# Two strip groups of the compression, and two levels of the gated recurrence, in one visit each of a hand-ordered matmul stream

## The chip, the cores and the metric

The kernel runs on one core of a Trainium2 chip, in one launch. The metric is the time of one execution on the device, in microseconds (us); less is better. Beside the times there is one profiled execution, whose records name every instruction by its engine, its line and its tiles.

## What is computed

A stack of two hybrid layers (three branches: sparse attention, gated linear attention, attention into a memory; then a gated merge and an MLP) and one further block, on 256 positions of width 1024, in float32. Two pieces of a hybrid layer matter here. The compression of the sparse attention's keys and values, cut to its core:

```python
raw = jnp.stack([split_heads(k_c, G), split_heads(v_c, G)])[:, :, :, cmp_idx]
raw = (raw + cmp_pe[:, None, None, None]).reshape(2, B, G, n_cmp, CMP_BLOCK * dh)
hid = jax.nn.gelu(jnp.einsum('kbgnf,kfe->kbgne', raw, cmp_w1))     # f is 2048, e is 256
comp = jnp.einsum('kbgne,ked->kbgnd', hid, cmp_w2)
```

and the attention matrix of the gated linear attention, in which each pair of positions i >= j is weighted by the decay between them:

```python
b = jnp.cumsum(ab, axis=2)
decay = jnp.exp(jnp.where(tril[:, :, None], b[:, :, :, None, :] - b[:, :, None, :, :], -jnp.inf))
attn = jnp.einsum('bhid,bhjd,bhijd->bhij', qb, kb, decay)
```

## The kernel before, in words

**The products.** A float32 product is made of three matmuls on a high and a low part of each operand (`mm3`, L194 and before it `mm`, L188, the one line that almost every matmul has in the trace). The weights stream from HBM in units of 512 KB: `unit` loads one into a raw buffer (tile `raw`, pool `wraw`, four buffers; the issue is on SP, L457), and `split` (L435 to L442) makes its high part `hi` on ACT (L441; every sixth unit on POOL, L439) and its low part `lo` on DVE (L442). The stationary operand of these products is the activation, the moving one a row block of weights 512 wide.

**The order on PE.** It is written by hand while the program is built. `tok_major` and `transposed` issue the big products; after each group of three matmuls they call `pump()`. All side work (recurrence, compression, scores, softmax products) is a set of generators, the chains. A chain issues a few instructions, then yields a number, the virtual time until it wants the next turn, a visit; `pump()` gives every chain whose time has come a visit, on a virtual clock that each matmul advances. So the numbers behind `yield` say where among the big products a visit falls. The order on ACT, DVE, POOL and SP is not written by hand: the framework's scheduler chooses it when the program is built. On every engine the instructions then run in their order, and a waiting instruction holds up all those behind it.

**The compression** (`nsa_cmp`, from L757). Tile `ph`, one bank of the pool `acc`, takes the product with `cmp_w1`. For each of two kinds (keys, values) there are four visits; each takes one raw buffer, fills it by two DMAs (L781) and issues four matmuls of 32 columns of stationary and 256 moving (L786), which occupy one strip of 32 columns each of the array. In a trace such a visit has eight records, since a float32 matmul goes in two passes. There are eight visits in each layer. These raw buffers come out of the same four as those of the big products, so a visit of the compression is what frees a buffer for a later weight unit.

**The gated recurrence** (`gla`, from L992). For each half of the positions (`tt`) ACT makes exponentials of prefix sums (PE products of `MLR` and `T` into a `psm` bank, L1021 on ACT into `E`, a `b8x` tile), DVE and POOL multiply keys and queries into them (L1025 to L1033 and `q_side`, L1048, which writes one of four tiles `QB`). Then come seven levels: each takes a bank of the pool `psm` (three banks, shared with every score, transpose and small product), issues two matmuls of 128 by 128 (four records) into its first half, and DVE copies the result under a mask into the matrix `A` (L1061); each level is a visit of its own. An eighth visit makes the diagonal (two matmuls of 2 columns, and the copy of L1073).

**What runs beside them.** In the stretch that matters most, the big products are first those of `gv` (columns 1816 to 2328 of `w_in`; their result is copied on ACT at L1286 into tile `g`), then those of `SR` (2328 to 2840, four weight units). Among them stand the first half of the recurrence, the compression, and the softmax of the sparse attention: scores on PE, a maximum on DVE (L899, L920), exponentials on ACT (L903, L924), normalisation on DVE (L905 to L929), transposes (L192 on PE).

Of the kernel before, what the change touches and what calls it, by code (L numbers as in the profile page):

```python
# [10 lines left out]
F32 = mybir.dt.float32  # L11
# [5 lines left out]
OP = mybir.AluOpType  # L17
AX = mybir.AxisListType.X

P = 128  # L20
# [18 lines left out]
CO_SEL = CO_TRIL  # L39
# [59 lines left out]
def block_kernel(ctx, tc, x_in, mem_in, positions, ln_mix, w_in, b_merge, nsa_q_norm, nsa_k_norm,  # L99
# [5 lines left out]
    nc = tc.nc  # L105
    act = nc.scalar.activation
    dve = nc.vector
    pool = nc.gpsimd

    consts = ctx.enter_context(tc.tile_pool(name="consts", bufs=1))  # L110
    wraw = ctx.enter_context(tc.tile_pool(name="wraw", bufs=NRAW))
# [10 lines left out]
    def nm(s):  # L122
        cnt[0] += 1
        return f"{s}_{cnt[0]}"

    LATF = 1.0
    clock = [0.0]
# [47 lines left out]
    def pe_time(ap, n):  # L175
        if ap.dtype == F32:
            return max(214.0, n * 1.69)
        return max(107.0, n * 0.425)

    def free(ap):  # L180
        n = 1
        for d in ap.shape[1:]:
            n *= d
        return n

    def mm(o, l, r, start, stop):
        clock[0] += pe_time(l, free(o))
        nc.tensor.matmul(o, l, r, start=start, stop=stop, skip_group_check=True)  # L188
# [35 lines left out]
    def A2(shape):  # L224
        return N2(shape, "a2")
# [10 lines left out]
    def PS():  # L236
        return psm.tile([P, 512], F32, tag="psm", name=nm("psm"))
# [7 lines left out]
    CF = consts.tile([P, CO_END], F32, name="CF")  # L245
# [17 lines left out]
    MASKS = consts.tile([P, MASK_W], U8, name="MASKS")  # L263
# [494 lines left out]
    def nsa_cmp(l, KD, GT, W2, T):  # L758
        R = [N2([P, 16, 2, 16]) for _ in range(2)]
# [13 lines left out]
        yield 3000.0  # L773
        ph = ACC()
        for k in range(2):
            for q in range(4):
                yield 3950.0
                raw = wraw.tile([P, 1024], F32, tag="raw", name=nm("raw"))
                rv = raw.rearrange("p (a n) -> p a n", a=4)
                for hl in range(2):  # L780
                    nc.sync.dma_start(rv[hl * 64:hl * 64 + 64],  # L781
                                      cmp_w1[l, k, hl * 1024 + q * 256:hl * 1024 + q * 256 + 256, :].rearrange(
                                          "(lp d) e -> d lp e", d=64))
                for j in range(4):
                    lp = 4 * q + j
                    nc.tensor.matmul(ph[32 * j:32 * j + 32, k * 256:k * 256 + 256],  # L786
                                     R[k][:, lp].rearrange("p a b -> p (a b)"), rv[:, j, :], start=q == 0,
                                     stop=q == 3, tile_position=(0, 32 * j), skip_group_check=True)
                clock[0] += 500.0
        cp = N2([P, 512])  # L790
        act(cp, ph, AF.Copy)
        yield 1500.0
# [1 line left out]
        for c in range(4):  # L794
# [4 lines left out]
                          op=OP.add, axis=AX)  # L799
# [186 lines left out]
    NQB = 4  # L986
    QB = [consts.tile([P, 2, 2, 64], F32, name=f"QB{i}") for i in range(NQB)]
# [3 lines left out]
    def gla(l, gq, gk, G, LOW, GLT, WG, o_gla, merged):  # L991
# [19 lines left out]
        for tt in range(2):  # L1011
            ts_ = slice(tt * P, tt * P + P)
            E = B8("b8x", shape=(2, 8, 128))
            for pr in range(2):
                for hf in range(2):
                    pd = PS()
                    rhs = MLR[:, 128 * tt + 512 * hf:128 * tt + 512 * hf + 512]
                    mm(pd, Th[:, tt, pr * P:pr * P + P], rhs, True, False)
                    mm(pd, Tl[:, tt, pr * P:pr * P + P], rhs, False, True)
                    yield 600.0  # L1020
                    act(E[:, pr, 4 * hf:4 * hf + 4, :].rearrange("p a b -> p (a b)"), pd, AF.Exp, scale=1.0 / 16)  # L1021
            for l2 in range(8):
                idx = l2 if tt == 0 else l2 + 1
                if idx == 0:
                    dve.tensor_tensor(KE, E[:, :, l2, :], gk[:, :, ts_], op=OP.mult)  # L1025
                elif idx == 8:
                    dve.tensor_tensor(E[:, :, l2, :], E[:, :, l2, :], gq[:, :, ts_], op=OP.mult)
                else:
                    s = 64 >> (idx - 1)
                    eng = dve if idx % 2 else pool  # L1030
                    e = E[:, :, l2, :].rearrange("p a (n u s) -> p a n u s", u=2, s=s)[:, :, :, 0, :]
                    q = gk[:, :, ts_].rearrange("p a (n u s) -> p a n u s", u=2, s=s)[:, :, :, 0, :]
                    eng.tensor_tensor(e, e, q, op=OP.mult)  # L1033
            yield 5350.0
            A = A2([P, 4, 128])
            AT.append(A)
            pool.memset(A, 0.0)

            def q_side(lev):
                sz = 64 >> (lev - 1)  # L1040
                qb = QB[(7 * tt + lev) % NQB]
                l2 = lev if tt == 0 else lev - 1
                eng = dve if lev % 2 else pool
                for j in range(2):
                    rr = slice(64 * j, 64 * j + 64)
                    e = E[rr, :, l2, :].rearrange("p a (n u s) -> p a n u s", u=2, s=sz)[:, :, :, 1, :]
                    q = gq[rr, :, ts_].rearrange("p a (n u s) -> p a n u s", u=2, s=sz)[:, :, :, 1, :]
                    eng.tensor_tensor(qb[rr, :, j, :].rearrange("p a (n s) -> p a n s", s=sz), e, q, op=OP.mult)  # L1048

            for lev in range(1, NQB + 1):  # L1050
                q_side(lev)
            for lev in range(1, 8):
                pa = PS()
                l2 = lev if tt == 0 else lev - 1
                qb = QB[(7 * tt + lev) % NQB]
                for pr in range(2):
                    mm(pa[:, pr * P:pr * P + P], E[:, pr, l2, :], qb[:, pr].rearrange("p j w -> p (j w)"),
                       True, True)
                sz = 64 >> (lev - 1)
                up_ = MASKS[:, None, 64 * (lev - 1):64 * lev].rearrange("p a (n s) -> p a n s", s=sz)  # L1060
                dve.copy_predicated(A.rearrange("p h (n u s) -> p h n u s", u=2, s=sz)[:, :, :, 1, :],  # L1061
                                    up_.to_broadcast([P, 4, 64 // sz, sz]),
                                    pa[:, 0:256].rearrange("p (h n s) -> p h n s", h=4, s=sz))
                if lev + NQB < 8:
                    q_side(lev + NQB)
                if lev == 1:
                    QK = E[:, :, l2, :]
                    pool.tensor_tensor(QK, gq[:, :, ts_], gk[:, :, ts_], op=OP.mult)
                yield 800.0
            pd = PS()  # L1070
            for pr in range(2):
                mm(pd[:, 2 * pr:2 * pr + 2], QK[:, pr, :], CF[:, CO_SEL:CO_SEL + 2], True, True)
            dve.copy_predicated(A, MASKS[:, None, 448:576].to_broadcast([P, 4, 128]),  # L1073
                                pd[:, 0:4, None].to_broadcast([P, 4, 128]))
            yield 1400.0
        Ac = A2([P, 4, 128])
        pas = [PS(), PS()]
# [32 lines left out]
        for hp in range(2):  # L1110
            pt = PS()
            for j in range(2):
                for tt in range(2):
                    h = 2 * hp + j
# [603 lines left out]
```

## Time and profile before

| | us |
|---|---|
| median of 3 runs | 1221.53 |
| the three runs | 1221.73, 1219.28, 1221.53 |
| the profiled execution, its own time | 1223.66 |
| span of its records | 1221.9 |
| PE busy (6553 matmul records) | 1201.4 |
| DVE busy | 871.5 |
| ACT busy | 605.1 |
| POOL busy | 199.5 |

A row of a timeline gives the start, the duration, the engine, the line, the operation with its tiles (numbers of buffers left out), the shapes, how many records stand together, and in brackets how long the engine had stood idle before it and what ended the wait. Matmuls overlap in the array: the pace of PE is read from one start to the next, not from the durations. Layer 1 shows the same pattern as layer 0, 472.0 us later.

### The profile page before, as it was taken

What the parts mean: (1) busy time and instruction counts of PE and PEld (TensorE: products, weight loads), DVE (VectorE), ACT (ScalarE), POOL (GpSimd) and SP (SyncE); (2) the same over time, 40 slices, a digit from 0 to 9 for tenths busy, and PEclk for the clock granted to TensorE, in tenths of its full rate; (3) what the DMA queues carried; (4) which work ended last, traced back from release to release, by engine and by line L of the source; (5) the groups of instructions that cost most, each with busy time, mean ns of one, the idle gap of its engine ahead of it and who ended that gap; (6) DMA issues with size and microseconds to landing.
All of it is one profiled execution on the core that took longest, in us unless ns stands there. A gap on an engine that the chain in (4) does not pass through costs nothing. (4 is left out here: it accounts for less than half of the span.)

```text
span 1221.9 us, 17759 instructions
## 1 busy us (share of the span) xinstructions
PE 1201.4 (98%) x6553; PEld 1004.8 (82%) x6553; DVE 871.5 (71%) x1457; ACT 605.1 (50%) x988; POOL 199.5 (16%) x235
## 2 busy tenths in 40 slices
PE   9999999999999999999999999999999999999997
PEld 6897777888788888888777888888888997998876
DVE  5977978677665656658868867665555799985677
ACT  7557544434645445466645444554554334443351
POOL 2310220120111112200312020121111111000201
PEclk9999999999999999999989999999999999999999
DMA  8567523676566666657613576656666555466662
GB/s 279 178 178 205 157 88 108 191 220 209 156 186 187 193 193 188 181 158 186 202 59 104 171 200 194 187 176 201 183 197 196 180 174 172 132 184 198 176 206 70
DMA packets 138699, 213.91 MB, mean 175 GB/s; under 512 B 12145, under 2 KB 76757, under 8 KB 138612
## 3 DMA queue, kind: packets, MB, share of 16 engines
q1 hardware_dynamic: 137284, 209.19, 57.8%
q0 software_dynamic: 1152, 3.31, 0.9%
q8 instruction: 51, 0.84, 0.3%
q14 instruction: 36, 0.29, 0.1%
q10 hardware_dynamic: 176, 0.27, 0.1%
HBM read 211.86 MB, written 1.05 MB: 174 GB/s over the span
## 5 line engine op out<-in xcount | busy, mean ns | idle before, releaser
L442 DVE TENSOR_TENSOR lo<-raw,hi 128x1024 fp32r<-128x1024 f32 (+1 forms) x369 | 458.6, 1246 | 219.9 <-ACT hi L441 169.4
L441 ACT ACTIVATE hi<-raw 128x1024 fp32r<-128x1024 f32 (+1 forms) x308 | 322.8, 1057 | 344.4 <-PE acc L188 284.5
L188 PE MATMUL acc<-hi,hx 128*128 128x512 f32 (+1 forms) x1024 | 338.3, 395 | 0.0
L188 PEld LDWEIGHTS acc<-hi,hx 128*128 128x128 f32 x1024 | 192.0, 189 | 40.2 <-issue 4.0
L188 PE MATMUL acc<-lo,hx 128*128 128x512 f32 (+1 forms) x512 | 197.3, 385 | 0.0
L439 POOL TENSOR_SCALAR hi<-raw 128x1024 fp32r<-128x1024 f32 x61 | 74.5, 1222 | 611.4 <-PE acc L188 438.5
L188 PE MATMUL acc<-hi,oh 128*128 128x512 f32 x400 | 157.9, 395 | 0.0
L188 PE MATMUL acc<-lo,oh 128*128 128x512 f32 x400 | 155.9, 390 | 0.0
L188 PE MATMUL acc<-hi,ol 128*128 128x512 f32 x400 | 155.8, 390 | 0.0
L188 PE MATMUL acc<-hx,hi 128*128 128x256 f32 (+1 forms) x704 | 137.7, 297 | 1.7 <-DVE hx L532 1.7
L188 PEld LDWEIGHTS acc<-hx,hi 128*128 128x128 f32 x704 | 110.9, 191 | 6.4 <-issue 2.3
L188 PE MATMUL psm<-hx,hi 128*128 128x512 f32 x448 | 111.8, 391 | 0.0
L188 PEld LDWEIGHTS acc<-lo,hx 128*128 128x128 f32 x512 | 96.9, 189 | 16.4
L188 PE MATMUL acc<-hi,b8x 128*128 128x512 f32 (+1 forms) x336 | 106.1, 388 | 1.4 <-ACT b8x L531 0.8
L188 PE MATMUL acc<-hx,lo 128*128 128x256 f32 x384 | 101.7, 284 | 0.3 <-DVE lo L442 0.3
L188 PEld LDWEIGHTS psm<-hx,hi 128*128 128x128 f32 x448 | 81.4, 189 | 15.1
L188 PEld LDWEIGHTS acc<-hi,ol 128*128 128x128 f32 x400 | 75.1, 188 | 15.9
L188 PEld LDWEIGHTS acc<-hi,oh 128*128 128x128 f32 x400 | 75.2, 188 | 14.7
L188 PEld LDWEIGHTS acc<-lo,oh 128*128 128x128 f32 x400 | 75.2, 188 | 14.6
L188 PEld LDWEIGHTS acc<-hi,b8x 128*128 128x128 f32 x336 | 62.3, 189 | 14.3 <-DVE b8x L532 1.5
L188 PEld LDWEIGHTS acc<-hx,lo 128*128 128x128 f32 x384 | 71.1, 191 | 1.5 <-DVE lo L442 0.5
L1351 POOL TENSOR_TENSOR tmp<-gtmp 128x512 f32<-128x512 f32 x32 | 39.1, 1223 | 165.7 <-ACT gtmp L1346 165.7
(359 smaller groups left out, 1464.4 us busy)
## 6 DMA issues: line engine op xcount, KB each, us to landing
raw<-in_w_in SPq DMA_DIRECT2D x160, 512.0 KB
raw<-in_w_up SPq DMA_DIRECT2D x64, 512.0 KB
raw<-in_w_down SPq DMA_DIRECT2D x64, 512.0 KB
raw<-in_w_branch SPq DMA_DIRECT2D x28, 512.0 KB
raw<-in_w_out SPq DMA_DIRECT2D x24, 512.0 KB
raw<-in_cmp_w SPq DMA_DIRECT2D x32, 256.0 KB
raw<-in_mem_w_kv SPq DMA_DIRECT2D x15, 512.0 KB
raw<-in_w_branch SPq DMA_DIRECT2D x16, 256.0 KB
```

The source lines that it names most:

```text
L188: nc.tensor.matmul(o, l, r, start=start, stop=stop, skip_group_check=True)
L439: pool.tensor_scalar(hi, raw, 1.0, 1.0, op0=OP.mult, op1=OP.mult)
L441: act(hi, raw, AF.Copy)
L442: dve.tensor_tensor(lo, raw, f32(hi), op=OP.subtract)
L1351: pool.tensor_tensor(u, r, r, op=OP.mult)
```

## The change

In the compression a visit now takes two raw buffers: it issues their four DMAs together, then the eight matmuls; a layer has four visits of eight matmuls in place of eight of four. The yield ahead of a visit becomes 8000 in place of 3950. In the recurrence the levels go in pairs (1, 2), (3, 4), (5, 6), and level 7 with the diagonal: a pair takes one `psm` bank, level 1 in its first half and level 2 in its second, then come the two masked copies one after the other; four visits in place of eight for each half, with yields of 1600, 1600, 1600 and 1400. The numbers of matmuls, copies and DMAs stay as they are.

```diff
--- before.py
+++ after.py
@@ -773,20 +773,24 @@
         yield 3000.0
         ph = ACC()
         for k in range(2):
-            for q in range(4):
-                yield 3950.0
-                raw = wraw.tile([P, 1024], F32, tag="raw", name=nm("raw"))
-                rv = raw.rearrange("p (a n) -> p a n", a=4)
-                for hl in range(2):
-                    nc.sync.dma_start(rv[hl * 64:hl * 64 + 64],
-                                      cmp_w1[l, k, hl * 1024 + q * 256:hl * 1024 + q * 256 + 256, :].rearrange(
-                                          "(lp d) e -> d lp e", d=64))
-                for j in range(4):
-                    lp = 4 * q + j
-                    nc.tensor.matmul(ph[32 * j:32 * j + 32, k * 256:k * 256 + 256],
-                                     R[k][:, lp].rearrange("p a b -> p (a b)"), rv[:, j, :], start=q == 0,
-                                     stop=q == 3, tile_position=(0, 32 * j), skip_group_check=True)
-                clock[0] += 500.0
+            for q2 in range(0, 4, 2):
+                yield 8000.0
+                rvs = []
+                for q in range(q2, q2 + 2):
+                    raw = wraw.tile([P, 1024], F32, tag="raw", name=nm("raw"))
+                    rv = raw.rearrange("p (a n) -> p a n", a=4)
+                    for hl in range(2):
+                        nc.sync.dma_start(rv[hl * 64:hl * 64 + 64],
+                                          cmp_w1[l, k, hl * 1024 + q * 256:hl * 1024 + q * 256 + 256, :].rearrange(
+                                              "(lp d) e -> d lp e", d=64))
+                    rvs.append(rv)
+                for q, rv in zip((q2, q2 + 1), rvs):
+                    for j in range(4):
+                        lp = 4 * q + j
+                        nc.tensor.matmul(ph[32 * j:32 * j + 32, k * 256:k * 256 + 256],
+                                         R[k][:, lp].rearrange("p a b -> p (a b)"), rv[:, j, :], start=q == 0,
+                                         stop=q == 3, tile_position=(0, 32 * j), skip_group_check=True)
+                clock[0] += 1000.0
         cp = N2([P, 512])
         act(cp, ph, AF.Copy)
         yield 1500.0
@@ -1049,29 +1053,33 @@
 
             for lev in range(1, NQB + 1):
                 q_side(lev)
-            for lev in range(1, 8):
+            for pair in ((1, 2), (3, 4), (5, 6), (7,)):
                 pa = PS()
-                l2 = lev if tt == 0 else lev - 1
-                qb = QB[(7 * tt + lev) % NQB]
-                for pr in range(2):
-                    mm(pa[:, pr * P:pr * P + P], E[:, pr, l2, :], qb[:, pr].rearrange("p j w -> p (j w)"),
-                       True, True)
-                sz = 64 >> (lev - 1)
-                up_ = MASKS[:, None, 64 * (lev - 1):64 * lev].rearrange("p a (n s) -> p a n s", s=sz)
-                dve.copy_predicated(A.rearrange("p h (n u s) -> p h n u s", u=2, s=sz)[:, :, :, 1, :],
-                                    up_.to_broadcast([P, 4, 64 // sz, sz]),
-                                    pa[:, 0:256].rearrange("p (h n s) -> p h n s", h=4, s=sz))
-                if lev + NQB < 8:
-                    q_side(lev + NQB)
-                if lev == 1:
-                    QK = E[:, :, l2, :]
-                    pool.tensor_tensor(QK, gq[:, :, ts_], gk[:, :, ts_], op=OP.mult)
-                yield 800.0
-            pd = PS()
-            for pr in range(2):
-                mm(pd[:, 2 * pr:2 * pr + 2], QK[:, pr, :], CF[:, CO_SEL:CO_SEL + 2], True, True)
-            dve.copy_predicated(A, MASKS[:, None, 448:576].to_broadcast([P, 4, 128]),
-                                pd[:, 0:4, None].to_broadcast([P, 4, 128]))
+                for i, lev in enumerate(pair):
+                    l2 = lev if tt == 0 else lev - 1
+                    qb = QB[(7 * tt + lev) % NQB]
+                    for pr in range(2):
+                        mm(pa[:, 256 * i + pr * P:256 * i + pr * P + P], E[:, pr, l2, :],
+                           qb[:, pr].rearrange("p j w -> p (j w)"), True, True)
+                if pair == (7,):
+                    for pr in range(2):
+                        mm(pa[:, 256 + 2 * pr:258 + 2 * pr], QK[:, pr, :], CF[:, CO_SEL:CO_SEL + 2], True, True)
+                for i, lev in enumerate(pair):
+                    sz = 64 >> (lev - 1)
+                    up_ = MASKS[:, None, 64 * (lev - 1):64 * lev].rearrange("p a (n s) -> p a n s", s=sz)
+                    dve.copy_predicated(A.rearrange("p h (n u s) -> p h n u s", u=2, s=sz)[:, :, :, 1, :],
+                                        up_.to_broadcast([P, 4, 64 // sz, sz]),
+                                        pa[:, 256 * i:256 * i + 256].rearrange("p (h n s) -> p h n s", h=4, s=sz))
+                    if lev + NQB < 8:
+                        q_side(lev + NQB)
+                    if lev == 1:
+                        QK = E[:, :, 1 if tt == 0 else 0, :]
+                        pool.tensor_tensor(QK, gq[:, :, ts_], gk[:, :, ts_], op=OP.mult)
+                if pair == (7,):
+                    dve.copy_predicated(A, MASKS[:, None, 448:576].to_broadcast([P, 4, 128]),
+                                        pa[:, 256:260, None].to_broadcast([P, 4, 128]))
+                else:
+                    yield 1600.0
             yield 1400.0
         Ac = A2([P, 4, 128])
         pas = [PS(), PS()]
```

How the built programs differ is seen on three engines at one place, in layer 0, where the products of `gv` end and those of `SR` begin. The lines of the changed kernel are shifted: L786 becomes L790, L1021 becomes L1025, L903 becomes L907, L924 becomes L928, L1286 becomes L1294.

On PE before, right behind the last products of `gv`: scores (`psm_1398`), a strip group of the compression (`acc_1066`), a product for the recurrence (`psm_1421`) and the first products of `SR` (`acc_1427`):

```order
L188 MATMUL psm_1398<-g_226_1219,b8x_1278 128x512
L188 MATMUL psm_1398<-g_227_1220,b8x_1278 128x512
L188 LDWEIGHTS CBT
L188 MATMUL psm_1398<-CBT 128x2x128
L786 MATMUL acc_1066<-raw_1413,n_192_1017 32x256 x4
L188 MATMUL psm_1421<-MLR,T_1270 128x512
L188 MATMUL psm_1421<-MLR,T_1271 128x512
L188 MATMUL acc_1427<-hi_1430,hx_135 128x512
L188 MATMUL acc_1427<-lo_1431,hx_135 128x512
```

and in the changed program:

```order
L188 MATMUL psm_1391<-g_226_1219,b8x_1271 128x512
L188 MATMUL psm_1391<-g_227_1220,b8x_1271 128x512
L188 LDWEIGHTS CBT
L188 MATMUL psm_1391<-CBT 128x2x128
L790 MATMUL acc_1066<-raw_1406,n_192_1017 32x256 x4
L790 MATMUL acc_1066<-raw_1409,n_192_1017 32x256 x4
L188 MATMUL psm_1421<-MLR,T_1263 128x512
L188 MATMUL psm_1421<-MLR,T_1264 128x512
L188 MATMUL acc_1427<-hi_1430,hx_135 128x512
L188 MATMUL acc_1427<-lo_1431,hx_135 128x512
```

Two strip groups stand together where one stood; the rest has its order. The fifth strip group of before, which stood 30 rows ahead of the one shown, is the first of the two here.

On ACT before, in the same stretch (`hi_1430` and `hi_1436` are the high parts of the first two units of `SR`, `pexp` the exponentials of the scores, `b8x` those of the recurrence, `g` the copies of `gv`):

```order
L751 ACTIVATE b8x_1278<-psm_1323,COL 128x4x128
L441 ACTIVATE hi_1430<-raw_1429 128x1024
L441 ACTIVATE hi_1436<-raw_1435 128x1024
L1021 ACT_TABLE_LOAD
L1021 ACTIVATE b8x_1369<-psm_1370 128x512
L903 ACTIVATE pexp_1355,s_248_1356<-psm_1346,n_246_1353 128x128 x4
L1021 ACTIVATE b8x_1369<-psm_1392 128x512
L924 ACTIVATE pexp_1382,s_256_1383<-psm_1376,n_254_1380 128x256 x2
L1286 ACTIVATE g_210_1182<-acc_1183,xrs_501 128x512
L1286 ACTIVATE g_210_1182<-acc_1184,xrs_501 128x512
L924 ACTIVATE pexp_1404,s_262_1405<-psm_1398,n_260_1402 128x256 x2
L441 ACTIVATE hi_1442<-raw_1441 128x1024
```

and in the changed program:

```order
L751 ACTIVATE b8x_1271<-psm_1323,COL 128x4x128
L1025 ACT_TABLE_LOAD
L1025 ACTIVATE b8x_1362<-psm_1363 128x512
L907 ACTIVATE pexp_1348,s_247_1349<-psm_1339,n_245_1346 128x128 x4
L1025 ACTIVATE b8x_1362<-psm_1385 128x512
L928 ACTIVATE pexp_1375,s_255_1376<-psm_1369,n_253_1373 128x256 x2
L1294 ACTIVATE g_210_1182<-acc_1183,xrs_501 128x512
L1294 ACTIVATE g_210_1182<-acc_1184,xrs_501 128x512
L928 ACTIVATE pexp_1397,s_261_1398<-psm_1391,n_259_1395 128x256 x2
L441 ACTIVATE hi_1430<-raw_1429 128x1024
L441 ACTIVATE hi_1436<-raw_1435 128x1024
L441 ACTIVATE hi_1442<-raw_1441 128x1024
```

The high parts of the first two units stood ahead of the table load and of all exponentials; they now stand behind them, with the third behind those two.

On DVE in the changed program, behind the normalisation of the scores (`pexp`; before, `lo_1431` stood ahead of the maximum of L899 and `lo_1437` ahead of the first of L920):

```order
L913 TENSOR_SCALAR pexp_1348<-pexp_1348,r_248_1354 128x128 x4
L924 TENSOR_REDUCE n_259_1395<-psm_1391 128x2
L930 RECIPROCAL r_256_1379<-s_255_1376 128x2
L931 TENSOR_TENSOR r_256_1379<-r_256_1379,GT_545 128x2
L933 TENSOR_SCALAR pexp_1375<-pexp_1375,r_256_1379 128x256 x2
L930 RECIPROCAL r_262_1401<-s_261_1398 128x2
L931 TENSOR_TENSOR r_262_1401<-r_262_1401,GT_545 128x2
L933 TENSOR_SCALAR pexp_1397<-pexp_1397,r_262_1401 128x256 x2
L442 TENSOR_TENSOR lo_1431<-raw_1429,hi_1430 128x1024
L442 TENSOR_TENSOR lo_1437<-raw_1435,hi_1436 128x1024
L442 TENSOR_TENSOR lo_1443<-raw_1441,hi_1442 128x1024
L442 TENSOR_TENSOR lo_1449<-raw_1447,hi_1448 128x1024
```

The low parts of the four units of `SR` now follow one another, behind the last normalisation. In layer 1 ACT has the same exchange, but for the first unit of `SR`, whose high part POOL makes before and now; its low part stands on DVE behind the first maximum and ahead of the normalisation.

## Rows read from the trace of the kernel before

**Rows 1.** The page, part 1: busy time, share of the span, instructions of each engine.

```profile
PE 1201.4 (98%) x6553; PEld 1004.8 (82%) x6553; DVE 871.5 (71%) x1457; ACT 605.1 (50%) x988; POOL 199.5 (16%) x235
```

**Rows 2.** The waits on PE: us in total, times, longest us.

```profile
PE psm L188 <- DVE a L1061: 2.1, 4, 1.3
...
PE psm L188 <- DVE tmp L798: 1.5, 2, 0.9
...
PE psm L192 <- DVE a L1061: 0.9, 1, 0.9
PE psm L192 <- DVE ck L834: 0.8, 1, 0.8
```

**Rows 3.** Timeline of PE, 114.4 to 116: start us, us, instruction, count of records.

```profile
114.40 0.40 PE L188 MATMUL acc<-hi,hx 128*128 128x512 f32 x1
114.73 0.64 PE L786 MATMUL acc<-raw,n 128*32 128x256 f32 x8
115.30 0.50 PE L188 MATMUL acc<-hi,hx 128*128 128x512 f32 x1
115.64 0.40 PE L188 MATMUL acc<-lo,hx 128*128 128x512 f32 x1
115.88 0.40 PE L188 MATMUL acc<-hi,hx 128*128 128x512 f32 x1
```

**Rows 4.** Timeline of PE: a level of the recurrence, and eight passes together.

```profile
137.34 0.61 PE L188 MATMUL psm<-QB,b8x 128*128 128x128 f32 x4
137.71 0.47 PE L188 MATMUL acc<-hi,hx 128*128 128x512 f32 x1
...
192.23 1.05 PE L188 MATMUL psm<-g,a 128*128 128x128 f32 x8
193.04 0.47 PE L188 MATMUL acc<-hi,hx 128*128 128x512 f32 x1
```

**Rows 5.** Timeline of PE, 119.5 to 121.9, where the products of SR begin.

```profile
119.54 0.39 PE L188 MATMUL acc<-hi,hx 128*128 128x512 f32 x1
...
120.22 0.28 PE L188 MATMUL psm<-CBT 128*128 128x256 bf16 x1
...
121.00 0.73 PE L188 MATMUL psm<-MLR,T 128*128 128x512 f32 x2
121.57 0.40 PE L188 MATMUL acc<-hi,hx 128*128 128x512 f32 x1
```

**Rows 6.** Timeline of ACT, 114 to 124.

```profile
114.03 2.00 ACT L441 ACTIVATE hi<-raw 128x1024 fp32r<-128x1024 f32 x2
...
118.00 0.36 ACT L903 ACTIVATE pexp<-psm,n 128x128 f32<-128x128 f32 x1
...
119.37 0.62 ACT L1021 ACTIVATE b8x<-psm 128x512 f32<-128x512 f32 x1
119.85 0.50 ACT L924 ACTIVATE pexp<-psm,n 128x256 f32<-128x256 f32 x1
...
120.75 1.31 ACT L1286 ACTIVATE g<-acc,xrs 128x512 f32<-128x512 f32 x2
121.89 0.53 ACT L924 ACTIVATE pexp<-psm,n 128x256 f32<-128x256 f32 x1
...
122.78 2.08 ACT L441 ACTIVATE hi<-raw 128x1024 fp32r<-128x1024 f32 x2
```

**Rows 7.** Timeline of DVE, 117 to 119.

```profile
117.64 1.22 DVE L442 TENSOR_TENSOR lo<-raw,hi 128x1024 fp32r<-128x1024 f32 x1
```

**Rows 8.** Line 1061 by itself: ns min/median/max, first and last start.

```profile
L1061 DVE COPY_PREDICATED a<-MASKS,psm x28: 416/432/741, 130.7 to 661.0; 128x256 f32<-128x256 uint8 x28
```

**Rows 9.** Timeline of PE, layer 1, the longest wait at a level.

```profile
652.33 0.68 PE L188 MATMUL psm<-QB,b8x 128*128 128x128 f32 x4 [1.25 <-DVE a L1061]
```

**Rows 10.** Stretches: us, busy time of PE, PEld, DVE, ACT, POOL; PEclk, DMA, GB/s.

```profile
631.00:638.00 7.00, 7.00 (x24) 4.93 (x24) 3.40 (x14) 1.50 (x3) 0.49 (x1) 0.52 0.01 2
638.00:675.00 37.00, 35.75 (x210) 28.68 (x210) 31.82 (x80) 19.99 (x46) 10.01 (x12) 1.00 0.31 92
```

## The prediction, made before the changed kernel ran

> **What bounds the kernel now.** I read the page first: PE is busy 98% of the span [rows 1], so the time is the length of PE's stream, and it changes only where PE issues something cheaper or dearer, or waits more or less. The page's chain of work that ended last covers only the last part of the span, so it says nothing on this change. Next the waits on PE: those that end at the recurrence and its neighbours are few, 2.1 us and 0.9 us for copies of levels (L1061), 1.5 us and 0.8 us for two vector operations of the compression (L798, L834) [rows 2]; 5.3 us in all for both layers. Then the timeline of PE at a visit of each kind, for its cost [rows 3, 4], and last the timelines of ACT and DVE where the new order differs most [rows 5 to 7]. Durations come from an execution whose own time was 1223.66 us (span 1221.9), 2.1 us above the median of 1221.53; I make a sum of differences and add it to the median. 0.2% is 2.4 us, about what a measurement of this kernel can tell from no change: 1219.1 and 1224.0 are the bounds.
>
> **Compression visits: -1.9 us.** Among plain products one start follows another after 0.24 us (115.64 to 115.88 [rows 3]). The visit at 114.73 comes 0.33 us after the start ahead of it, takes 0.57 us to the next start, and that product then needs 0.34 us [rows 3]: 0.09 + 0.57 + 0.10 = 0.76 us. Two visits cost 1.52 us. Merged, entry and exit are paid once: 0.19 saved. If an end of the last sweep, which is in the 0.57, is also paid once, and is of the size of the entry, 0.28 is saved. I take 0.24 for each of eight mergers in the two layers, -1.9 us, with ends -1.5 and -2.3. The DMAs stay the same in number and in SP's order; what changes is when a buffer comes free (below).
>
> **Recurrence visits: 0.** A level costs 0.37 us for four records to the next start, and that product runs some 0.08 long; eight records in a row cost 0.81 us [rows 4]. So two visits are 2 x 0.45 = 0.90, and a merged one 0.81 + 0.08 = 0.89. Sixteen banks saved save no PE time by themselves. Ends: 1 us either way, for neighbours that now meet. The vector copies are the same 28, of 0.43 us [rows 8], and 4 for the diagonal.
>
> **The wait that the change brings: +2.7 us in layer 0.** The raw buffers of the first units of SR come free when the compression has used them. Now two strip groups go together, so the first unit's buffer, which the third group frees before, is freed with the fourth, and the third unit's with the sixth instead of the fifth. The build answers by another order: the first two high parts, which ran on ACT at 114.03, in a gap ahead of the exponentials [rows 6], stand behind the exponentials, the two copies of gv and the last exponentials. ACT does its work in order, so SR waits for all of these. Step by step: three visits before this place (two mergers, and the group at 114.73, which is gone to the next visit) move the stream forward by 2 x 0.24 + 0.76 = 1.24 us. The exponentials hang on PE's scores, so they start at 118.00 - 1.24 = 116.8. From there to the last exponential ACT needs 122.78 - 118.00 = 4.78 us without a gap [rows 6], each of its sources being 1.24 us earlier too (the last products of gv, 119.54, and the last score, 120.22 [rows 5]). That is 121.5 or 121.6. The high part takes half of 2.08 us [rows 6]: 122.6. The low part on DVE takes 1.22 us [rows 7]: 123.8. PE wants the high part where SR starts, at 121.57 [rows 5] - 1.24 + 0.52 (the merged visit is 0.76 - 0.24 longer than one group) = 120.85, and the low part one product later. So it waits 1.75 us for the high part and, one product further, about 1.0 more for the low one: 2.7 us. The later units follow at 1.0 on ACT and 1.22 on DVE each, faster than PE uses one (twelve products of 0.24, 2.9 us), so they wait no more. Ends: 4.0 if ACT's block isn't pulled forward by the 1.24 us, and 0 if its exponentials run two to three microseconds ahead of my reckoning. I stay at 2.7, as PE's scores fix the start of the block.
>
> **The same place in layer 1: +0.2 us.** There POOL makes the first high part, and its low part is ahead of the normalisation. The second unit comes by the same reckoning at 122.6 for its high and 123.8 for its low part, on layer 0's scale (there the two copies of gv stand ahead of both score exponentials, which changes the order and not the sum). PE wants them 2.9 us and one more product for the recurrence (121.57 - 121.00 = 0.57 [rows 5]) after 120.85, at 124.3. Nothing or little is lost; ends 0 and 1.0.
>
> **The waits at the levels: 0.** The 5.3 us [rows 2] are banks and vector results that come late from DVE. Half as many banks are asked for, but each is held for two copies, with what DVE does between them. I see no reason for one to outweigh the other; ends -2.8 (half goes) and +4.3 (the rival below). PE being 2.7 us later in layer 0 gives DVE time there, yet DVE has four low parts in a row to make first.
>
> Sum: -1.9 + 0 + 2.7 + 0.2 + 0 = +1.0 us, **1222.5 us**.
>
> **The rivals.** *The waits shrink (faster).* If the exponentials run ahead so that SR waits only 1.0 us, and half of the waits at levels go with half of the banks, the sum is -1.9 + 1.0 + 0.2 - 2.8 = -3.5 us: 1218.0. For it: ACT is free of 2.00 us of high parts at 114.03 and DVE of a low part at 117.64 between its maxima [rows 6, 7]. Against it: the start of ACT's block is set by PE, not by ACT. Chance 0.22.
>
> *The shared bank is late (slower).* Waits for L1061 are five now, 3.0 us [rows 2]. A pair's bank comes free one masked copy later, and the build puts normalisations and a query product between the two copies. If each of the five waits grows by a copy and as much again, 2 x 0.43 [rows 8], that is +4.3, 1226.8. It decides from the point where PE asks for the third bank after a pair before DVE has done both copies; the longest wait, 1.25 us in layer 1 [rows 9], shows that DVE is that late at one place already. For it: DVE has four low parts in a row ahead of the first half's levels. Against it: only five waits stand behind 28 copies now [rows 2, 8], and half as many banks are asked for. Chance 0.20.
> The Trainium skill (Perfetto Trace Analysis, Optimizing Tensor Performance, Matmuls) says that independent groups of matmuls should rotate through different PSUM banks, so that the evacuation of one overlaps the matmuls of the next; two levels in one bank go against it. By that rule alone the time would be this rival's. The trace agrees in part: its waits for L1061 are waits for banks [rows 2], but most of the 28 copies [rows 8] held nobody up. So this rival has half the chance of the forecast.
>
> *The clock falls after the new gap (slower).* After the small matmuls of layer 1 the granted clock is 0.52, the level of 1.2 GHz, for 7.0 us, and 1.00 again after that [rows 10]: 3.4 us lost. If the gap of 2.7 us ahead of SR brings half to one such stretch, 1222.5 + 1.7 to + 3.4, 1224.2 to 1225.9. Against it: the clock is 1.00 over the stretch from 638 that holds the wait of 1.25 us [rows 9, 10]. Chance 0.10.
>
> *The merger doesn't merge (slower).* If the second strip group of a visit waits for its own DMA, or four strips on the next buffer begin anew, entry and exit are paid twice and the 1.9 us don't come: 1222.5 + 1.9 = 1224.4. Chance 0.08. The forecast keeps 0.40.
>
> **How the numbers follow.** The forecast lies within 0.2% of 1221.53: same, 0.40. The first rival is faster: 0.22. The others are slower: 0.20 + 0.10 + 0.08 = 0.38. The low end, 1217.8, stands just below the price of the faster rival, which leaves out its lower half, 0.11; the high end, 1227.0, just above the price of the late bank, which leaves out its upper half, 0.09.
>
> **What would show it right or wrong.** Right: the visit of the compression has 16 records within some 1.14 us and four visits in a layer; ACT's high part of SR's first unit follows the last exponentials of the scores; the first two products of SR in layer 0 stand with waits for ACT's L441 and DVE's L442, together 2 to 4 us, and layer 1 has no such pair; waits for the copies of levels (now L1070) stay near 3 us. Wrong: no wait at the first product of SR in layer 0; waits for L1070 above 6 or below 1 us; a row of PEclk near 0.5 right after the start of SR.

## The result, and the profile after

The changed kernel takes 1232.55 us (median of 4 runs, 1230.0 to 1234.11) against 1221.63 for the kernel before beside it: a ratio of 1.0075, 95% interval 1.0057 to 1.0094. It is slower by some 11 us, and the forecast was 1222.5, with a range up to 1227.0. Slower had the chance of 0.38, but the size was far off. The profiled execution has a span of 1230.8 us, 8.9 more than before; its account is made below.

The page of the changed kernel, part 1, answers to [rows 1]:

```profile
PE 1203.1 (98%) x6553; PEld 1007.5 (82%) x6553; DVE 871.1 (71%) x1457; ACT 604.8 (49%) x988; POOL 192.4 (16%) x235
```

PE has the same 6553 records and still 98% of the span. The waits on PE in the changed kernel (us in total, times, longest us), answering to [rows 2], leaving out waits outside the two hybrid layers' attention stages:

```profile
PE psm L192 <- ACT b8x L1025: 3.1, 1, 3.1
PE psm L192 <- DVE pexp L933: 2.5, 2, 1.2
PE acc L188 <- ACT hi L441: 1.8, 1, 1.8
...
PE psm L192 <- ACT pts L945: 1.7, 2, 0.9
PE psm L188 <- ACT n L813: 1.3, 2, 1.1
...
PE acc L188 <- DVE lo L442: 1.2, 3, 0.8
...
PE psm L188 <- DVE a L1070: 0.7, 3, 0.3
PE pso L188 <- ACT pts L674: 0.7, 1, 0.7
...
PE psm L192 <- DVE ck L838: 0.6, 1, 0.6
PE psm L188 <- ACT b8x L1025: 0.5, 2, 0.2
```

Waits for the masked copies of the levels were 3.0 us (L1061 [rows 2]) and are 0.7 now (L1070). What came instead are waits for ACT (L1025, L441, L945, L813) and for normalised exponentials from DVE (L933). The ten rows make 14.1 us; 0.4 of the row for L442 lies elsewhere, so 13.7 stand in the two stages, where before there were 5.6 ([rows 2], and one of 0.3 for L941).

The place in layer 0 that the prediction worked out, on PE and on ACT (timelines; [rows 5, 6] before):

```profile
120.06 0.28 PE L188 MATMUL psm<-CBT 128*128 128x256 bf16 x1
120.28 1.07 PE L790 MATMUL acc<-raw,n 128*32 128x256 f32 x16
121.28 0.74 PE L188 MATMUL psm<-MLR,T 128*128 128x512 f32 x2
123.81 0.50 PE L188 MATMUL acc<-hi,hx 128*128 128x512 f32 x1 [1.79 <-ACT hi L441]
125.06 0.50 PE L188 MATMUL acc<-lo,hx 128*128 128x512 f32 x1 [0.76 <-DVE lo L442]
```

```profile
117.84 0.36 ACT L907 ACTIVATE pexp<-psm,n 128x128 f32<-128x128 f32 x1
...
121.73 0.53 ACT L928 ACTIVATE pexp<-psm,n 128x256 f32<-128x256 f32 x1
...
122.62 2.07 ACT L441 ACTIVATE hi<-raw 128x1024 fp32r<-128x1024 f32 x2
```

The visit has 16 records in 1.00 us. PE comes here a microsecond later than reckoned, in part by a wait of 0.7 us for L674 in the stretch ahead, and with it the exponentials (117.84, forecast 116.8) and the high part (122.62, forecast 121.6); the first two products of SR wait 1.79 and 0.76 us. That is the 2.7 of the forecast, at 2.55.

In layer 1 the start of SR has no such wait, but another follows some four microseconds behind it. ACT, PE and SP there:

```profile
598.60 2.08 ACT L441 ACTIVATE hi<-raw 128x1024 fp32r<-128x1024 f32 x2
603.66 1.06 ACT L441 ACTIVATE hi<-raw 128x1024 fp32r<-128x1024 f32 x1 [2.98 <-DMA raw<-in_w_in]
604.62 1.06 ACT L1025 ACTIVATE b8x<-psm 128x512 f32<-128x512 f32 x2
```

```profile
601.71 0.49 PE L192 MATMUL psm<-CF,pexp 128*128 128x128 f32 x3
605.25 0.90 PE L192 MATMUL psm<-CF,pexp 128*128 128x128 f32 x3 [3.05 <-ACT b8x L1025]
```

```profile
586.47 10.86 SPq L457 DMA_DIRECT2D raw<-in_w_in  x4
597.43 4.85 SPq L783 DMA_DIRECT2D raw<-in_cmp_w  x4
```

ACT makes the high parts of SR's second and third unit at 598.60 and is then to make the fourth. Its transfer is the last of the four that SP issues by 597.33 (586.47 + 10.86), right ahead of four transfers of the compression; it lands at 603.66, when ACT's wait for it ends. ACT waits 2.98 us for it. Behind it in ACT's order stand the two copies out of PSUM banks for the recurrence (L1025 at 604.62). The transposes on PE need one of the three banks, and wait 3.05 us for the copy to free it.

The transfer is late because its buffer is. Before, SP had issued the same four units by 588.48, 5.0 us ahead of SR's first product at 593.46:

```profile
575.94 12.54 SPq L457 DMA_DIRECT2D raw<-in_w_in  x4
```

Now the last goes out by 597.33, 0.5 us ahead of SR's first product at 597.83. SP issues the third unit at 594.84, after a wait for the first unit's own low part (L442), and the fourth at 596.96, after a wait of 1.7 us for the merged visit of 596.26 (L790). In layer 0 it waits 9.5 us for such a visit ahead of the third.

The third part is the granted clock (stretches, columns as in [rows 10]). Of the changed kernel:

```profile
122.00:126.00 4.00, 1.45 (x6) 0.99 (x6) 3.27 (x7) 3.84 (x8) 0.00 (x0) 1.00 0.79 261
126.00:131.00 5.00, 5.00 (x27) 4.17 (x26) 4.90 (x9) 2.33 (x4) 4.36 (x6) 1.00 0.93 206
160.00:168.00 8.00, 8.00 (x33) 5.97 (x33) 5.33 (x21) 2.30 (x10) 1.14 (x2) 0.57 0.20 66
596.00:602.00 6.00, 6.00 (x40) 4.39 (x39) 5.60 (x17) 4.68 (x12) 0.00 (x0) 1.00 0.96 250
604.00:612.00 8.00, 6.75 (x23) 4.83 (x23) 5.30 (x11) 2.06 (x4) 4.70 (x8) 0.57 0.56 158
642.00:646.00 4.00, 4.00 (x15) 2.38 (x15) 2.90 (x13) 2.30 (x10) 1.14 (x2) 0.58 0.32 117
```

and the first low stretch of the kernel before, whose second one is in [rows 10]:

```profile
159.90:163.40 3.50, 3.50 (x13) 2.23 (x13) 1.95 (x9) 1.40 (x3) 0.00 (x0) 0.52 0.00 0
```

Before, 3.5 and 7.0 us at 0.52 cost 10.5 x 0.48 = 5.0 us. Now it is 8 us at 0.57, 8 at 0.57 and 4 at 0.58: 8.6 us lost, 3.6 more. The one from 604 is new, and begins within PE's wait of 3.05 us.

So the profiled execution adds up: 13.7 - 5.6 = +8.1 of waits, +3.6 of clock, and the merged visits of the compression, 0.33 us for each of eight (1.00 instead of 2 x 0.57 inside, and the 0.19 of one entry and exit, an estimate taken over from before), -2.6. Sum +9.1, against 8.9. Two things stand outside this sum: the other waits of PE are 1.0 us less in all (one of 0.8 us for L531 is gone), and the first 1.25 us of the low stretch from 604 lie within PE's wait, so that some 0.5 us is counted twice. With both, 7.6 of the 8.9 us are accounted for.

### The profile page after: what moved, and what is told of

The parts are those of the page before. It is cut to its first block, busy times and chain, and to the rows that moved or that the text cites. A ratio compares the mean times of both kernels' runs of the same rounds, so it can differ in the third digit from the quotient of the medians.

```text
span 1230.8 us, 17763 instructions
## 1 busy us (share of the span) xinstructions
PE 1203.1 (98%) x6553; PEld 1007.5 (82%) x6553; DVE 871.1 (71%) x1457; ACT 604.8 (49%) x988; POOL 192.4 (16%) x235
## 5 line engine op out<-in xcount | busy, mean ns | idle before, releaser
L442 DVE TENSOR_TENSOR lo<-raw,hi 128x1024 fp32r<-128x1024 f32 (+1 forms) x369 | 458.3, 1245 | 230.2 <-ACT hi L441 177.2
L441 ACT ACTIVATE hi<-raw 128x1024 fp32r<-128x1024 f32 (+1 forms) x308 | 322.7, 1057 | 349.7 <-PE acc L188 287.9
L188 PEld LDWEIGHTS acc<-hi,b8x 128*128 128x128 f32 x336 | 62.4, 189 | 13.7 <-DVE b8x L532 1.5
```

The source lines that it names most:

```text
L441: act(hi, raw, AF.Copy)
L442: dve.tensor_tensor(lo, raw, f32(hi), op=OP.subtract)
```

## The experiments

Each execution's records give its span and its mean granted clock. To tell waits from clock I put beside each median the mean of span x granted clock over the runs of that kernel, an estimate of the time that it would take at the full clock. The kernel before ran again beside each group, and each ratio is to the kernel before of its own group.

| kernel | median us | ratio to before, interval | mean granted clock | span x clock, us |
|---|---|---|---|---|
| before (35 runs beside the third group) | 1222.49 | | 0.9959 | 1215.6 |
| changed, once more | 1230.50 | 1.0064 (1.0050 to 1.0079) | 0.9928 | 1219.7 |
| pairs of levels alone | 1224.29 | 1.0011 (1.0001 to 1.0021) | 0.9947 | 1216.0 |
| pairs of strip groups alone | 1228.25 | 1.0040 (1.0027 to 1.0053) | 0.9934 | 1218.6 |
| changed, pairs of groups early | 1225.93 | 1.0023 (1.0007 to 1.0039) | 0.9945 | 1217.8 |
| early pairs of groups alone | 1227.67 | 1.0036 (1.0024 to 1.0049) | 0.9948 | 1219.9 |
| changed, one high part of layer 1 on POOL | 1230.01 | 1.0069 (1.0052 to 1.0085) | 0.9923 | 1219.6 |
| changed, one of layer 0 on POOL | 1231.69 | 1.0070 (1.0054 to 1.0086) | 0.9903 | 1218.2 |
| changed, both on POOL | 1230.25 | 1.0061 (1.0042 to 1.0080) | 0.9937 | 1220.3 |
| outer pairs of groups alone | 1223.01 | 1.0009 (0.9994 to 1.0023) | 0.9958 | 1216.0 |
| outer pairs of groups, pairs of levels | 1221.62 | 0.9991 (0.9977 to 1.0005) | 0.9952 | 1213.9 |
| changed, five raw buffers | 1218.36 | 0.9977 (0.9966 to 0.9989) | 0.9958 | 1212.0 |
| before, five raw buffers | 1223.83 | 1.0020 (1.0009 to 1.0030) | 0.9939 | 1214.9 |
| pairs of groups alone, five raw buffers | 1220.95 | 0.9984 (0.9975 to 0.9993) | 0.9954 | 1213.6 |
| pairs of levels alone, five raw buffers | 1223.54 | 0.9998 (0.9989 to 1.0007) | 0.9964 | 1216.9 |

Theory A: the pairs of strip groups free the buffers of SR's weight units late, so splits and transfers come late, and engines that work in order hold other work up behind them. Theory B, the rival of the prediction: the shared bank of two levels makes the waits.

### The halves of the change

Each half alone: the loop of the other is that of the kernel before.

```diff
-            for pair in ((1, 2), (3, 4), (5, 6), (7,)):
+            for lev in range(1, 8):
...
```

> The pairs of levels alone; the compression as before. Theory A (the loss comes from the paired strip groups, which free the weight buffers later, so that splits move behind other work on ACT and DVE): no wait at the first product of SR, no 3 us wait for L1021 in layer 1, time within 2 us of before (1219.5 to 1223.5). Theory B (the shared bank of two levels, held for two copies, makes the waits): most of the loss is here, 1227 to 1232, with the waits at transposes and small products of the first half of the recurrence as in the changed kernel (together over 5 us a layer).

> The paired strip groups alone; the levels of the recurrence one by one as before. Theory A: all or most of the loss is here, 1228 to 1233, with waits of 1.8 and 0.8 us at the start of SR in layer 0 and some 3 us for L1025 in layer 1. Theory B: little of it, 1219 to 1224.

The pairs of levels cost 1.0 us (before was 1223.29 in this set), the pairs of groups 5.0. Waits on PE of the pairs of groups alone:

```profile
PE psm L188 <- DVE a L1065: 3.4, 4, 1.2
PE psm L188 <- ACT ck L831: 2.2, 2, 1.7
...
PE acc L188 <- ACT hi L441: 1.8, 1, 1.8
```

Theory A holds for the larger part: the wait of 1.8 us at the start of SR is there with the pairs of groups alone. The wait of 3 us for L1025 in layer 1 is not (0.5 us); there other small waits stand, for L1065 and L831. The halves don't add up either: 1.0011 and 1.0040 against 1.0064 to 1.0075. Theory B is refuted as the main cause.

### Earlier visits

```diff
-                yield 8000.0
+                yield 4000.0 if k == 0 and q2 == 0 else 8000.0
```

> The changed kernel, but with the first of the four paired strip visits of a layer 4000 instead of 8000 of virtual time after its predecessor, so that a pair stands about where the first of its two groups stood before and its two weight buffers come free earlier, not later. Theory A: the waits at the start of SR and for L1025 in layer 1 go, and with them 6 us or more: 1220 to 1226. Theory B: the levels are paired as in the changed kernel, so it stays at 1229 to 1234.

> The paired strip groups alone, at the early places; levels one by one. Theory A: the merger's saving of some 2 us without the waits, 1217 to 1221. Theory B: the same as before less 2 us, 1218 to 1221, and 8 us or more below the early pairs with paired levels.

With the levels in pairs the waits at the start of SR are gone and the time is 1225.93, at the upper end of what theory A said; with the levels one by one it is 1227.67, far above its 1217 to 1221. Theory B's 1218 to 1221 is missed there too. So theory A in this form is not enough. The early visits seem only to have turned the late buffer round, as the waits on PE of the second show:

```profile
PE acc L790 <- DMA raw<-in_cmp_w: 3.0, 2, 1.9
PE psm L192 <- DVE ck L838: 2.4, 2, 1.9
```

Now the visit itself is early for its own transfers (3.0 us in two waits), since its two buffers must be free at one time, and the chain behind the compression is late (2.2 us for L802 and 2.4 for L838, where the kernel before has 1.5 and 0.8 for the same lines, L798 and L834 [rows 2]).

### The changed kernel again, and single instructions moved

The first run repeats the changed kernel. The others move one high part each to POOL:

```diff
-        if u % 6 == 5:
+        if u % 6 == 5 or u == 176:
```

Unit 176 is SR's fourth in layer 1; u == 30 is SR's first in layer 0; both together are the fourth run.

> The changed kernel once more, for a second profile and beside the next three on one chip. If the 3 us wait for L1025 in layer 1 and the stretch of low granted clock that begins in it belong to the program, both are there again, and the time is 8 to 11 us above before. If the stretch of low clock was chance, the wait is there without it and the time is 5 to 8 us above before.

> The changed kernel with one instruction moved: the high part of SR's fourth unit in layer 1 is made on POOL instead of ACT, so that ACT no longer waits for that unit's transfer ahead of the copy out of the PSUM bank. Order of PE and DVE unchanged. If this convoy on ACT makes the 3 us wait: the wait for L1025 falls below 0.5 us, the time by 3 us, and by 3 more where the low clock came with the gap: 3 to 7 us below the changed kernel. If PE would wait there anyway (for the low part of the unit, or the bank through another holder): within 1 us of it.

> The changed kernel with the high part of SR's first unit in layer 0 on POOL, as layer 1 has it; the build then puts its low part ahead of the normalisation on DVE. If the place behind ACT's exponentials makes the wait at the start of SR: the waits of 1.8 and 0.8 us go and the time falls by 2 to 3 us. If the unit's transfer is what is late, the wait stays, on POOL's L439: within 1 us.

> Both moves. If the two waits are separate pieces of the loss: 5 to 9 us below the changed kernel, 1 to 5 above before. If the loss moves on to later waits (DVE and ACT behind): less than 3 us below the changed kernel.

The repeat is 7.8 us above before (1222.72 in this set), just under the 8 to 11 expected, and its wait for L1025 and its low clock in layer 1 are there again, both somewhat smaller:

```profile
PE psm L192 <- ACT b8x L1025: 2.3, 1, 2.3
```

```profile
604.00:608.50 4.50, 3.65 (x11) 3.04 (x12) 4.13 (x9) 1.66 (x4) 3.48 (x6) 0.62 0.99 266
```

None of the three moves gains anything clear of the noise. With the fourth unit of layer 1 on POOL, the wait of 3 us for L1025 is gone, and another takes its place. Waits on PE, then POOL and DVE:

```profile
PE pso L188 <- DVE pts L947: 2.4, 1, 2.4
```

```profile
604.48 1.04 POOL L439 TENSOR_SCALAR hi<-raw 128x1024 fp32r<-128x1024 f32 x1 [11.32 <-DMA raw<-in_w_in]
```

```profile
605.55 1.47 DVE L442 TENSOR_TENSOR lo<-raw,hi 128x1024 fp32r<-128x1024 f32 x1 [1.90 <-POOL hi L439]
```

POOL now waits for the transfer (until 604.48), DVE for POOL's high part (1.90 us, until 605.55), and a copy behind that on DVE's order (L947) is what PE waits for. So ACT was only the engine that happened to carry the late transfer; the transfer is the cause of this wait. With SR's first unit of layer 0 on POOL the waits of 1.8 and 0.8 us go, and waits for L1025 and L813 come in the same layer (over both layers, on PE):

```profile
PE psm L192 <- ACT b8x L1025: 4.2, 2, 2.9
PE psm L188 <- ACT n L813: 2.8, 2, 1.7
```

In this kernel ACT makes the fourth unit's high part ahead of the copy L1025 in layer 0 too. The loss moves on: theory A's first, narrow reading, that two instructions stand at the wrong place, falls. The reading left is that buffers come free late, and somebody waits wherever the splits are put.

### Which pairs, and more buffers

Only groups 1 and 2, and 7 and 8 in pairs; 3 to 6 single, as their visits free SR's buffers:

```diff
-            for q2 in range(0, 4, 2):
-                yield 8000.0
+            for qs in (((0, 1), (2,), (3,)), ((0,), (1,), (2, 3)))[k]:
+                yield 8000.0 if len(qs) == 2 else 3950.0
```

> Levels one by one as before. Of the eight strip groups of a layer only 1 and 2, and 7 and 8 go in one visit; 3 to 6, whose visits free the buffers of SR's units, stay single. If late buffers make the loss: no wait at the start of SR, none for L1025 in layer 1, and the time is that of before less some 1 us (four mergers): 1220 to 1223 beside a before of 1222.7. If any merged visit costs (its two buffers, its DMAs, the mode change), half of the loss of the paired strip groups stays: 1225 or more.

> The same with the levels in pairs as in the changed kernel. If late buffers make the loss and the pairs of levels cost about 1 us: 1222 to 1225. If the pairs of levels and the pairs of strip groups make their waits together: 1227 or more.

Both come out near before (1223.01 and 1221.62, beside 1222.49). The wait at the start of SR and the one of 3 us for L1025 are gone, the loss with them; in layer 1 SR's four units are issued by 591.1 and 590.8. Beside these the pairs of levels cost nothing; the second is 1.4 us lower, within the noise of the two ratios. The gain of 1 us expected of the outer pairs is not there; PE waits for the transfers of two of their visits, as the first kernel shows:

```profile
PE acc L790 <- DMA raw<-in_cmp_w: 2.4, 2, 1.4
```

Five raw buffers instead of four, with the room taken from two other rings, in the changed kernel and, as control, in the kernel before:

```diff
-NRAW = 4
+NRAW = 5
...
-... bufs={"pexp": 4}.get(tag, 2))
+... bufs={"pexp": 3, "gtmp": 1}.get(tag, 2))
```

> The changed kernel with five raw buffers instead of four; room for it is made by one buffer less of the exponentials of the scores (three of four) and one less of the gate's temporary (one of two). The first three units of SR then load and split before the exponentials, as before. If late buffers make the loss: waits at the start of SR and for L1025 in layer 1 gone, and not more than 3 us above the same kernel before with five buffers. If not: 6 us or more above that.

> The kernel before with the same five raw buffers and the same two buffers less: the control of the run ahead. Within 3 us of before either way; lower if the loads of SR and of the gate's units bound it, higher if the smaller rings of exponentials or temporaries wait.

The same change is now a gain: 1218.36, 2.3 per mille below before, and below its control at 1223.83 by 5.5 us. Nothing of the change was undone. In its trace ACT makes the first three high parts of SR ahead of the exponentials again, and SR's products follow one another (ACT, then PE):

```profile
113.87 1.05 ACT L441 ACTIVATE hi<-raw 128x1024 fp32r<-128x1024 f32 x1
...
115.70 1.05 ACT L441 ACTIVATE hi<-raw 128x1024 fp32r<-128x1024 f32 x1
117.63 1.06 ACT L441 ACTIVATE hi<-raw 128x1024 fp32r<-128x1024 f32 x1 [0.88 <-DMA raw<-in_w_in]
```

```profile
123.84 0.73 PE L188 MATMUL psm<-MLR,T 128*128 128x512 f32 x2
124.41 0.39 PE L188 MATMUL acc<-hi,hx 128*128 128x512 f32 x1
124.64 0.39 PE L188 MATMUL acc<-lo,hx 128*128 128x512 f32 x1
```

In layer 1 SR's four units are issued by 590.04 again, 6.5 us ahead of its first product at 596.59:

```profile
577.34 12.70 SPq L457 DMA_DIRECT2D raw<-in_w_in  x4
```

So the loss was mainly the late buffers. Not every wait of the changed kernel goes: one of 1.0 us for L1025 stands in layer 0, and the 2.5 us for L933 are there as before the fifth buffer, so these are not the buffers' doing. The control by itself is 2.4 us slower than before by its ratio, so the fifth buffer, at this price in other rings, is worth nothing without the change; its waits for the masked copies are 3.8 us. The two smaller rings were not run without the fifth buffer.

The halves with five buffers:

> The paired strip groups alone, with five raw buffers (and the two buffers less of the runs before). If the pairs of strip groups gain their merger, some 2.6 us, once the buffers aren't late: 2 to 4 us below the control with five buffers. If the gain of the whole change there (5.5 us) comes from the pairs of levels: within 1.5 us of the control.

> The pairs of levels alone, with five raw buffers. If a shared bank saves waits for banks: 1.5 to 4 us below the control with five buffers, with the control's 3.8 us of waits for the masked copies below 1.5. If it only moves them: within 1.5 us of the control.

By the ratios to the kernel before, 1.0020 for the control, 0.9984 and 0.9998, the pairs of groups gain 0.36% on the control (4.4 us) and the pairs of levels 0.22% (2.7 us), each with some 0.15% either way; the control was not run in the set of the two halves, so this goes by way of the kernel before in both. Both together gain 0.43%. So the pairs of groups seem to be the larger half of the gain, as they were of the loss, though the two intervals overlap. For the pairs of levels the two measures disagree: their span x clock is 2 us above the control's, and their mean granted clock is higher. Their waits for the copies of the levels did not fall below the 1.5 us expected; they are 3.3 us, and 1.3 more for the copy of the diagonal.

## Why the prediction was wrong, point by point

| term | forecast us | found in the profiled execution us |
|---|---|---|
| merged visits of the compression | -1.9 | -2.6 |
| merged visits of the recurrence | 0 | 0 |
| wait at the start of SR, layer 0 | +2.7 | +2.6 |
| same stretch, layer 1 | +0.2 | +3.1 |
| other waits in the two stages | 0 | +2.4 |
| granted clock | 0 | +3.6 |

**What held.** The price of the merged visit, a little low; the pairs of levels save nothing on PE (two timings of a merged visit of the recurrence, to be compared with 0.81 for eight records in [rows 4]):

```profile
135.67 1.16 PE L188 MATMUL psm<-QB,b8x 128*128 128x128 f32 x8
136.58 0.48 PE L188 MATMUL acc<-hi,hx 128*128 128x512 f32 x1
...
138.75 1.06 PE L188 MATMUL psm<-QB,b8x 128*128 128x128 f32 x8
139.57 0.47 PE L188 MATMUL acc<-hi,hx 128*128 128x512 f32 x1
```

0.91 and 0.82 us to the next start. And the wait at the start of SR, by its mechanism and its size, from the timelines of before and the order alone; PE and ACT both came 1.0 us later than reckoned, which leaves the wait between them as it was.

**The step that failed** is the sentence "The later units follow at 1.0 on ACT and 1.22 on DVE each, faster than PE uses one ..., so they wait no more", and with it "Nothing or little is lost" for layer 1. I had followed the split's place in the order, but took the data of the later units as there. The working named the cause itself, the third unit's buffer being freed with the sixth group instead of the fifth, and then gave no time to the transfers behind it. In layer 1 SP has issued the four units only 0.5 us ahead of SR's first product, where before it was 5.0. The fourth unit's is issued by 597.33 and lands at 603.66, 6.3 us, with the DMA engines 0.96 busy at 250 GB/s from 596 to 602, as the compression's own transfers follow it. And I had not asked what stands behind a waiting high part on ACT: the copy that frees a PSUM bank.

**"The waits at the levels: 0"** was too narrow a term. The copies' own waits fell by 2.3 us (3.0 to 0.7), as the faster rival said and below the 1 us that the prediction had named as a sign of being wrong, but the term took in only these. (Half of its 5.3 us is 2.65, not the 2.8 that the working took.) Other results of ACT and DVE came late to PE, as waits for L933, L945 and L813, 5.5 us together, where before there was only one of 0.3 us at such a line (L941).

**The rivals.** The shared bank did not come true in the changed kernel: L1070 holds PE up less than L1061 did. The clock came true, by a path next to the one that I gave: the low stretch followed the gap in layer 1, not the one ahead of SR (122 to 131 is at 1.00 above). With a price of 1.7 to 3.4 us it was about the right size, 3.6 us, and had a chance of 0.10. The Trainium skill's rule on rotating through banks (Perfetto Trace Analysis, Optimizing Tensor Performance, Matmuls), by which the rival's time would have come, does not explain the loss: waits for the shared bank went down from 3.0 to 0.7 us. For the pairs of levels alone the waits are mixed: 2.1 us, the diagonal included, with four buffers, and with five 4.6 against the control's 3.8.

**Still open.** Why the halves cost 1.0 and 5.0 us apart and 8 to 11 together is explained only in part: the wait of 3 us in layer 1 exists in the whole change alone, though with the pairs of groups alone the fourth unit is issued as late (by 598.24). The 2.5 us for L933 also come only where both kinds of pairs stand together (none with the outer pairs; only 0.9, at another place, with the early ones), with four buffers as with five; why is not shown. What the pairs of levels are worth by themselves is not settled; it was +1.0 us alone with four buffers, -1.4 beside the outer pairs, and with five buffers -2.7 by the ratios and +2.0 by span x clock. Which gap brings a stretch of low clock is open too. The mean granted clock of the changed kernel is 0.9910 and 0.9928 in two sets of runs against 0.9959, 4 to 6 us of its loss by the estimate above; with most of its waits away (five buffers) it is 0.9958.

## What to carry to other kernels

A visit that uses two buffers of a shared ring at once frees both late and wants both early: before merging, list who takes the freed slot next, and follow that transfer to its landing and to what stands behind its first reader on an in-order engine. A wait that disappears when one instruction is moved, and comes back under another engine's name with the time unchanged, points past the engines to the data. Test a merger that loses with one more buffer before dropping it: here the same change went from 0.7% slower to 0.2% faster than the kernel before.

## What the runs showed of the hardware that was not expected

The granted clock can fall within a wait of PE and stay low after it: 0.57 over 604 to 612, with PE waiting from about 602.2 to 605.25 and busy from then on, at about the level of 1.2 GHz; the repeat has it again, 0.62 from 604 to 608.5. The same kind of wait doesn't always do it. Behind the wait at the start of SR the changed kernel has 1.00 (122 to 131), while the pairs of groups alone have, with the same wait, from 125 on:

```profile
125.00:129.00 4.00, 4.00 (x13) 3.11 (x12) 4.00 (x5) 2.12 (x4) 3.16 (x3) 0.58 0.73 184
```

The changed kernel with layer 1's fourth unit on POOL has the same waits there as the changed kernel, and 0.66 over 126 to 131. So the same stall is followed by a low stretch in one execution and not in another. Where one follows, the rows give a loss of some 1.7 us (4 us at 0.58) to 3.4 us (8 at 0.57) beyond the stall of 2.6 to 3.05 us itself. That the stall brings it about isn't shown: the stretches at 160 and 642 come with PE busy throughout.
